# Attention of a decoder trunk: the causal mask inside the row pass, and GpSimd for the scaling of the weights

## The chip, the core and the metric

The kernel is one program on one core of a Trainium2 chip. The metric is the device time of one execution in microseconds (us). A core has five engines with a queue each: TensorE (matmuls; PE in the profile, its weight loads PEld), VectorE (DVE), ScalarE (ACT), GpSimd (POOL) and SyncE (SP), which here issues the transfers. They work in their own order and wait for each other at semaphores. SBUF is the memory on the chip, PSUM the banks that TensorE writes its sums to.

## The reference, cut to what matters

512 tokens of 1024 features go through a Mamba-2 layer and an attention layer, each followed by a SwiGLU mixer. The attention has 16 query heads of 64 features on four shared heads of keys and values, with three branches: compressed blocks, selected blocks and a window. With 512 tokens the selection takes all blocks and the window all keys, so both are causal softmax attention, on keys and values of their own:

```python
s = einsum("bqhgd,bhqnkd->bhgqnk", qr, ks) * scale
p = masked_softmax(s, tok <= t)            # selected blocks
o_sel = einsum("bhgqnk,bhqnkd->bqhgd", p, vs)
...
p = masked_softmax(s, wmask)               # window
o_win = einsum("bhgqk,bkhd->bqhgd", p, vw)
o = g[..., 0:1] * o_cmp + g[..., 1:2] * o_sel + g[..., 2:3] * o_win
```

`g` are gates per token, head and branch. All is float32.

## The kernel before

The work is written in a tile language. A planner orders the instructions of VectorE, GpSimd and SyncE by its own costs; in the attention loop the orders of TensorE and ScalarE are those of the program text (`manual_schedule`).

The loop runs over 32 units (t, b): eight pairs of heads t, and for each the four tiles b = 3, 2, 1, 0 of 128 queries. A query tile b has n = 128 (b + 1) keys, since later ones are masked. A unit has four rows of scores per query: two heads on two branches. In `nsa`, one turn of the loop does this, in TensorE's order:

- `scores` of the next unit: per bank two matmuls (high and low part of the queries, L995 and L996), then a matmul that adds the mask of the last 128 keys (L998; the mask is a bfloat16 tile of 0 and -1e30 times the identity). VectorE takes the negated extreme of each row (L1000), ScalarE the exponential with the row's sum (L1005). For b = 3 and 2 a bank holds one row of scores (`per` is 1), for b = 1 two, for b = 0 all four.
- `turn_over` of this unit: TensorE transposes the weights (L1036) to PSUM, in two parts; VectorE copies the first part back (L1042), ScalarE the second (L1040). Two PSUM banks (`mi`) serve all turns, so the second part waits for the copies of the first.
- between the two parts, `av` of the unit before: the weights times the values (L1053), and after b = 0 the compressed branch (L888).
- some steps of `queries` of the pair t + 2 (`fills`: 1, 1, 2 and 5 steps of three matmuls for b = 3, 2, 1, 0), which end with the rotation: a shuffle (L705) and products on VectorE (L708), a product on GpSimd (L706), a sum (L710), the high part on ScalarE (L712), the low part on VectorE (L714). Then four transfers spread the result over the partitions (L844), and `scores` of (t + 1, 3) waits for them.
- `normalise` of the next unit: reciprocal of the sums (L1011), times the gates (L1013), then the four scalings of the weights (L1016), all on VectorE.
- for even t, steps of `compressed`, with matmuls of their own (L943).

Of the kernel before, what the change touches and what calls it, by code (L numbers as in the profile page):

```python
# [9 lines left out]
F32 = mybir.dt.float32  # L10
# [4 lines left out]
OP = mybir.AluOpType  # L15
# [25 lines left out]
class Weights:  # L41
    """A matrix as a stream of 128x128 blocks, eight to a transfer, each split exactly in two."""
# [21 lines left out]
    def held(self):  # L64
        """The next eight blocks, to be kept for longer."""
        assert self.left == 0
        hi, lo = self.kern.split_unit(self.dram[self.unit], held=True)
        self.unit += 1
        return [(hi[:, i * P:(i + 1) * P], lo[:, i * P:(i + 1) * P]) for i in range(8)]


class Kernel:
# [19 lines left out]
    def banks(self, n, i=0):  # L92
        """n banks to accumulate in; of two or four, the ones of i differ."""
        if n == 2:
            return [self.acc(), self.acc()] if i == 0 else [self.seg(), self.seg()]
        return [self.acc() for _ in range(min(n, N_ACC))] + [self.seg() for _ in range(n - N_ACC)]
# [11 lines left out]
    def split(self, hi, lo, src, bias=None):  # L108
        """hi + lo is src (+ bias) with all of its bits, each part exact in float32r."""
        nc = self.nc  # L110
        if bias is None:
            nc.scalar.activation(hi, src, AF.Copy)  # L112
            nc.vector.tensor_tensor(out=lo, in0=src, in1=hi.bitcast(F32), op=OP.subtract)  # L113
        else:
            nc.scalar.activation(hi, src, AF.Identity, bias=bias)
            nc.vector.scalar_tensor_tensor(out=lo, in0=src, scalar=bias, in1=hi.bitcast(F32),
                                           op0=OP.add, op1=OP.subtract)
# [19 lines left out]
    def linear(self, weights, x, ps=None):  # L137
        """One tile of 128 output features; x is a list of (hi, lo) per input tile."""
        ps = self.acc() if ps is None else ps
        for k, (xh, xl) in enumerate(x):  # L140
            wh, wl = weights.next()
            self.mm3(ps, wh, wl, xh, xl, k == 0, k == len(x) - 1)
        return ps

    def linear_start(self, weights, x, count, parts):
        """The first tiles of output features, token part by token part, as their inputs come."""
        pss = self.banks(count)
        ws = [weights.held() for _ in range(count)]
        for sl in parts:
            for ps, w in zip(pss, ws):  # L150
                for k, (xh, xl) in enumerate(x):
                    self.mm3(ps[:, sl], w[k][0], w[k][1], xh[:, sl], xl[:, sl], k == 0, k == len(x) - 1)
        return pss

    def mod(self, n, behind=False):
        """Modulation columns 128 n.. : silu(c) @ mod_w + mod_b."""
        nc = self.nc
        raw = self.rawp.tile([P, 1024], F32, name="raw")
        nc.sync.dma_start(raw, self.a["mod"][n])
        i = nc.vector.scalar_tensor_tensor(out=raw, in0=raw, scalar=1.0, in1=self.cs, op0=OP.mult, op1=OP.mult,  # L160
                                           accum_out=self.modc[:, n:n + 1])
        if behind:
            self.tc.keep_in_program_order(i)
        nc.vector.tensor_tensor(out=self.modc[:, n:n + 1], in0=self.modc[:, n:n + 1],
                                in1=self.col("mod_b", n), op=OP.add)
# [8 lines left out]
    def scale_cols(self, gain, mod0, plus):  # L174
        """gain * (plus + modulation) as columns."""
        o = self.const.tile([P, KD], F32, name=f"sc_{gain[0]}_{gain[1]}")
        self.nc.vector.scalar_tensor_tensor(out=o, in0=self.mod_cols(mod0), scalar=float(plus),
                                            in1=self.col(gain[0], gain[1], KD), op0=OP.add, op1=OP.mult)
        return o

    def rsqrt(self, sums, n):
        """1 / sqrt(sums / n + eps) of a few columns."""
# [20 lines left out]
    def rstd(self, sums, n):  # L203
        """1 / sqrt(mean + eps) of sums of squares [feature lane, token], on all partitions, in PSUM."""
        nc = self.nc
        ps = self.mi()
        for t in range(4):
            nc.tensor.matmul(ps[:, t:t + 1], sums[:, t * P:(t + 1) * P], self.ones[:, 0:1], start=True, stop=True)
        y = self.rsqrt(ps[:, 0:4], n)
        ps = self.mi()  # L210
        for t in range(4):
            nc.tensor.transpose(ps[:, t * P:(t + 1) * P], y[:, t:t + 1].to_broadcast([P, P]), self.ident)
        return ps

    def unit_rows(self, x, out):
        """out[t] = x[t] * rstd, for a few tiles of tokens [token, feature]; written over with squares before."""
# [16 lines left out]
    def turned(self, xn, k, count=1):  # L233
        """Feature tiles k.. of rows, with features on partitions, in PSUM."""
# [8 lines left out]
    def modulate(self, h, src, scale, shift, k, sl):  # L243
        """h = (hi, lo) of src * scale + shift."""
# [8 lines left out]
    def rows(self, cols):  # L253
        """Columns of features as rows of 1024, on all partitions."""
# [17 lines left out]
    def mm3_rows(self, ps, x, t, wh, wl, start, stop):  # L272
        """Adds to ps, [token, 512 features], what input tile x gives for token tile t."""
# [6 lines left out]
    def project_out(self, dram, x, x_src, gain, x_dst, first=None, after=None, mods=(), held=()):  # L280
        """x_src + gain * rmsnorm(x @ weights), [token, feature]. The second half of the features is done in two
        token parts, and what follows on a part (after) goes on while the other is multiplied. Without first, both
        halves of the features are."""
# [29 lines left out]
        for i in range(2):  # L313
# [19 lines left out]
            # one token tile ends before the other  # L333
# [62 lines left out]
    def before(self, gain, mod0, keep=None):  # L396
        """What follows on the residual stream: the modulated norm, to go on with; and its tiles."""
# [46 lines left out]
    def conv(self, ps, j):  # L444
        """Causal convolution of four taps of channel tile j."""
# [8 lines left out]
    def steps(self, ps, c):  # L454
        """softplus, cumulated decays and what hangs on them, from the raw steps [32 heads, tokens]."""
# [139 lines left out]
    def ssd(self, g, bt, ct, xs, w, h, c, zs):  # L595
        """The eight heads of group g: [2 heads x 64, tokens] tiles, gated and normalised."""
        nc = self.nc
        # C B per chunk: [source, target] blocks (0,0) (0,1) of each chunk, then (1,1) of each
# [15 lines left out]
        # tokens on partitions: steps times x, and with the decay to the end of chunk 0  # L614
# [84 lines left out]
    def rope(self, ps, factor, flat, out):  # L699
        """Rotated 512 tokens of two heads to out; flat gets the unrotated ones."""  # L700
# [16 lines left out]
    def compress_in(self, ps, t, t2):  # L717
        """Two heads' tokens to [(token parity, feature), head, token pair]."""
# [7 lines left out]
    def compress_blocks(self, t2, which):  # L726
        """The blocks with their position embedding, split: per half of their rows [row lane, row, head, block]."""
# [14 lines left out]
    def compress(self, blocks, which, c):  # L742
        """silu(blocks @ w1) as [hidden, 2, (head, block)], blocks with their position embedding."""
# [15 lines left out]
    def nsa(self, came, x_src, x_dst):  # L759
        nc = self.nc  # L760
        hk, xt = came
        with ExitStack() as es:
# [3 lines left out]
            nc.vector.tensor_copy(out=self.mask_q, in_=c("mask_q"))  # L766
            rot = self.big()
# [8 lines left out]
            # keys and values  # L776
# [36 lines left out]
            # gates  # L813
# [13 lines left out]
            # queries, two heads at a time  # L827
# [107 lines left out]
    def compressed(self, flat, kc, gates, kv, c, o):  # L935
        """Gated weights of the compressed blocks for the four heads of kv: [(head, block), query]."""
# [33 lines left out]
    def scores(self, qs, ks, t, b):  # L970
        """Unnormalised causal weights [query, key] of the queries of tile b, of two heads on both branches."""
# [12 lines left out]
        for j in range(4 // per):  # L984
            bank = self.seg()
            for i in range(j * per, (j + 1) * per, min(per, 2)):
# [9 lines left out]
                nc.tensor.matmul(v, q[:, 1, bs], k, start=False, stop=False, skip_group_check=True)  # L996
                for x in ([v[:, 0], v[:, 1]] if per > 1 else [v]):
                    nc.tensor.matmul(x[:, n - P:n], self.identb, self.mask_q, start=False, stop=True,  # L998
                                     skip_group_check=True)
            nc.vector.tensor_reduce(nm[:, j * per:(j + 1) * per],  # L1000
# [7 lines left out]
    def normalise(self, unit, gates, t, b):  # L1008
# [6 lines left out]
        for i, p in enumerate(unit["p"]):  # L1015
            nc.vector.tensor_scalar(p, p, d[:, i:i + 1], None, op0=OP.mult)  # L1016

    def turn_over(self, unit, b, part):
        """Weights with keys on partitions; part 0 by VectorE, part 1 by ScalarE."""
# [26 lines left out]
    def weigh(self, po, unit, vt, t, b, first):  # L1046
        """Adds to po what the queries of tile b get, for the heads 2 t and 2 t + 1."""
# [54 lines left out]
def _cols(v):  # L1102
    """A vector as columns of 128."""
# [3 lines left out]
def _blocks(w, order):  # L1107
    """Blocks (k, n) of w in that order, eight to a unit: [unit, 128, 8 * 128]."""
# [12 lines left out]
def _halves(w):  # L1121
    """Blocks of a half of the columns after the other's."""
# [3 lines left out]
def _rows(w, width):  # L1126
    """Row tiles of w, each [128, n], put side by side to units of 1024 columns."""
# [59 lines left out]
```

## Time and profile before

| | us |
|---|---|
| runs shown | 1564.48, 1565.19, 1568.77 (median 1565.19) |
| span of the profiled execution | 1564.4 |
| TensorE busy | 1515.3 (97%) |
| VectorE busy | 989.5 (63%) |
| ScalarE busy | 701.9 (45%) |
| GpSimd busy | 20.4 (1%) |
| attention loop, in the span | 937 to 1140 |

The span runs from the first to the last instruction of the profiled execution; its own device time is not listed beside it, and the runs are other executions. Busy time is a share over stages with different limits, so what a change in the loop is worth has to be read from the loop. Matmuls overlap in their pipeline and their ends are modelled, so starts are safer to read than durations. "x4" in a timeline merges four instructions.

### The profile page before, as it was taken

The page shows a single profiled execution, that of the slowest core. Times are in us where ns is not written, and L with a number is a line of the kernel's source. Part 1 is how long each engine was busy: PE and PEld are TensorE (multiplying, and loading weights), DVE is VectorE, ACT ScalarE, POOL GpSimd, SP SyncE. Part 2 cuts the span into 40 slices and gives each one's busy share as a digit, 9 for nine tenths or more (in the row PEclk, how much of TensorE's full clock was granted, in tenths as well). Part 3 has the DMA queues.
Part 4 walks back from the last instruction along what each step waited for, and adds up shares of the span by engine and source line. Part 5 has one row for each costly group of instructions (what it writes and reads, how often), then busy time and mean ns, then how long its engine had stood idle before and what let it go on. Part 6 is the DMA issues. An engine that isn't in the chain of part 4 may idle for free.

```text
span 1564.4 us, 20765 instructions
## 1 busy us (share of the span) xinstructions
PE 1515.3 (97%) x8014; PEld 1216.9 (78%) x8014; DVE 989.5 (63%) x1800; ACT 701.9 (45%) x1228; POOL 20.4 (1%) x27
## 2 busy tenths in 40 slices
PE   6999999999999999999999989999999999999997
PEld 4767676777889788888878877777688888888886
DVE  7856676778585788872367578888856333333246
ACT  4564746565364222322356465655645332222243
POOL 0000000000000000000000100000000000000000
PEclk9999999999999999999999999999999999999999
DMA  8422141334763888873466443122144122232254
GB/s 303 152 68 68 41 135 46 117 121 156 257 211 109 280 296 285 297 269 101 167 215 210 108 149 94 48 75 68 42 175 149 41 95 94 95 106 95 95 202 148
DMA packets 65125, 226.11 MB, mean 145 GB/s; under 512 B 7809, under 2 KB 9345, under 8 KB 65026
## 3 DMA queue, kind: packets, MB, share of 16 engines
q1 hardware_dynamic: 64738, 224.53, 43.5%
q8 instruction: 63, 1.03, 0.3%
q14 instruction: 36, 0.29, 0.1%
q10 hardware_dynamic: 288, 0.25, 0.1%
HBM read 204.83 MB, written 8.39 MB: 136 GB/s over the span
## 4 chain that ended last, share of the span: by engine, by line
PE 77%; DVE 9%; DMA 8%; ACT 3%; issue 2%; SPq 1%; POOL 0%; DVEq 0%; ACTq 0%; POOLq 0%
PE acc L133 12%; PE acc L134 12%; PE acc L135 12%; PE seg L276 5%; PE seg L278 5%; PE seg L277 5%; PE acc L278 3%; PE acc L276 3%; PE acc L277 3%; DMA raw<-in_mod_dram 2%; DMA raw<-in_ffn_in_dram 2%; DVE w L113 2%; PE mi L1036 2%; DMA b<-b 2%; PE acc L1053 2%
## 5 line engine op out<-in xcount | busy, mean ns | idle before, releaser
L113 DVE TENSOR_TENSOR w<-raw,w 128x1024 fp32r<-128x1024 f32 x233 | 288.0, 1237 | 260.0 <-ACT w L112 259.3
L112 ACT ACTIVATE w<-raw 128x1024 fp32r<-128x1024 f32 x233 | 245.9, 1057 | 369.4 <-PE seg L278 120.5
L133 PE MATMUL acc<-b,w 128*128 128x512 f32 x976 | 386.0, 397 | 3.2 <-DVE t L450 1.0
L134 PE MATMUL acc<-b,w 128*128 128x512 f32 x976 | 384.0, 393 | 0.0
L135 PE MATMUL acc<-b,w 128*128 128x512 f32 x976 | 383.5, 393 | 0.1
L133 PEld LDWEIGHTS acc<-b,w 128*128 128x128 f32 x976 | 183.3, 188 | 43.1 <-issue 4.1
L135 PEld LDWEIGHTS acc<-b,w 128*128 128x128 f32 x976 | 183.7, 188 | 39.8 <-issue 1.7
L134 PEld LDWEIGHTS acc<-b,w 128*128 128x128 f32 x976 | 183.8, 188 | 36.9 <-issue 0.7
L160 DVE SCALAR_TENSOR_TENSOR raw<-raw,b 128x1024 f32<-128x1024 f32 x112 | 136.1, 1221 | 19.1 <-DMA raw<-in_mod_dram 18.4
L276 PE MATMUL seg<-w,b 128*128 128x512 f32 x340 | 132.9, 391 | 0.0
L278 PE MATMUL seg<-w,b 128*128 128x512 f32 x340 | 132.7, 390 | 0.0
L277 PE MATMUL seg<-w,b 128*128 128x512 f32 x340 | 132.4, 389 | 0.0
L1005 ACT ACTIVATE b<-seg,nm 128x512 f32<-128x512 f32 (+3 forms) x128 | 66.0, 525 | 52.5 <-DVE nm L1000 49.8
L112 ACT ACTIVATE b<-t 128x512 fp32r<-128x512 f32 (+1 forms) x108 | 55.2, 529 | 47.8 <-DVE t L426 38.5
L277 PEld LDWEIGHTS seg<-w,b 128*128 128x128 f32 x340 | 63.8, 188 | 13.3
L278 PEld LDWEIGHTS seg<-w,b 128*128 128x128 f32 x340 | 63.8, 188 | 13.2
L276 PEld LDWEIGHTS seg<-w,b 128*128 128x128 f32 x340 | 63.9, 188 | 12.7
L426 DVE TENSOR_TENSOR t<-t,acc 128x512 f32<-128x512 f32 x40 | 27.4, 685 | 63.3 <-PE acc L135 63.3
L425 ACT ACTIVATE t<-acc 128x512 f32<-128x512 f32 x40 | 23.7, 593 | 95.3 <-PE acc L135 95.3
L113 DVE TENSOR_TENSOR b<-t,b 128x512 fp32r<-128x512 f32 (+1 forms) x108 | 59.2, 567 | 9.2 <-ACT b L112 8.9
L277 PE MATMUL acc<-w,b 128*128 128x512 f32 x164 | 64.0, 390 | 0.0
L278 PE MATMUL acc<-w,b 128*128 128x512 f32 x164 | 64.0, 390 | 0.0
(300 smaller groups left out, 2390.1 us busy)
## 6 DMA issues: line engine op xcount, KB each, us to landing
raw<-in_mod_dram SPq DMA_DIRECT2D x112, 512.0 KB, 4.5
raw<-in_ffn_in_dram SPq DMA_DIRECT2D x88, 512.0 KB, 4.5
raw<-in_ffn_out_dram SPq DMA_DIRECT2D x66, 512.0 KB, 3.3
raw<-in_ssm_in_dram SPq DMA_DIRECT2D x41, 512.0 KB, 3.4
raw<-in_ssm_out_dram SPq DMA_DIRECT2D x24, 512.0 KB, 4.3
b<-b SPq DMA_DIRECT2D x32, 256.0 KB, 4.5
raw<-in_kv_dram SPq DMA_DIRECT2D x12, 512.0 KB, 4.2
raw<-in_q_dram SPq DMA_DIRECT2D x9, 512.0 KB, 5.5
```

The costliest lines, as they stand in the source:

```text
L112: nc.scalar.activation(hi, src, AF.Copy)
L113: nc.vector.tensor_tensor(out=lo, in0=src, in1=hi.bitcast(F32), op=OP.subtract)
L133: nc.tensor.matmul(ps, wh, xh, start=start, stop=False)
L134: nc.tensor.matmul(ps, wh, xl, start=False, stop=False)
L135: nc.tensor.matmul(ps, wl, xh, start=False, stop=stop)
L160: i = nc.vector.scalar_tensor_tensor(out=raw, in0=raw, scalar=1.0, in1=self.cs, op0=OP.mult, op1=OP.mult, accum_out=self.modc[:, n:n + 1])
L276: nc.tensor.matmul(ps, x[0][:, ts], wh, start=start, stop=False)
L277: nc.tensor.matmul(ps, x[0][:, ts], wl, start=False, stop=False)
L278: nc.tensor.matmul(ps, x[1][:, ts], wh, start=False, stop=stop)
L1005: nc.scalar.activation(p[i], bank[:, at:at + n], AF.Exp, bias=nm[:, i:i + 1], accum_out=d[:, i:i + 1])
L1036: nc.tensor.transpose(ps[:, i * n + a * P:i * n + (a + 1) * P], unit["p"][j * per + i][:, a * P:(a + 1) * P], self.ident)
L1053: self.nc.tensor.matmul(po[64 * i:64 * i + 64, bs], vt[a][:, r * 256 + kv * 64:r * 256 + kv * 64 + 64], unit["w"][2 * i + r][:, a * P:(a + ...
```

## The change

For the query tiles b = 3 and 2, the mask's matmul is left out. One instruction of VectorE, `tensor_tensor_reduce`, replaces the reduction: it reads the scores in PSUM and a mask of 512 columns in SBUF (zeros, and the triangle in the last 128 columns), adds them, negates the sum, writes it to SBUF in the place of the weights, and takes the smallest of the row. ScalarE's exponential then works in place on SBUF with a scale of -1. Tiles b = 1 and 0 keep mask and reduction. In `normalise` of all tiles, the scaling of the weights goes from VectorE to GpSimd. The wide mask is built once, by GpSimd. The diff also strips comments and docstrings, left out here.

```diff
@@ nsa
             nc.vector.tensor_copy(out=self.mask_q, in_=c("mask_q"))
+            self.mask_w = keep.tile([P, 512], F32, name="mask_w")
+            nc.gpsimd.memset(self.mask_w[:, 0:384], 0.0)
+            nc.gpsimd.tensor_copy(out=self.mask_w[:, 384:512], in_=c("mask_q"))
@@ scores
                 nc.tensor.matmul(v, q[:, 0, bs], k, start=at == 0, stop=False, skip_group_check=True)
-                nc.tensor.matmul(v, q[:, 1, bs], k, start=False, stop=False, skip_group_check=True)
-                for x in ([v[:, 0], v[:, 1]] if per > 1 else [v]):
+                nc.tensor.matmul(v, q[:, 1, bs], k, start=False, stop=per == 1, skip_group_check=True)
+                for x in ([v[:, 0], v[:, 1]] if per > 1 else []):
                     nc.tensor.matmul(x[:, n - P:n], self.identb, self.mask_q, start=False, stop=True,
                                      skip_group_check=True)
+            if per == 1:
+                nc.vector.tensor_tensor_reduce(out=p[j], in0=bank[:, 0:n], in1=self.mask_w[:, 512 - n:512],
+                                               scale=-1.0, scalar=3.0e38, op0=OP.add, op1=OP.min,
+                                               accum_out=nm[:, j:j + 1])
+                nc.scalar.activation(p[j], p[j], AF.Exp, bias=nm[:, j:j + 1], scale=-1.0, accum_out=d[:, j:j + 1])
+                continue
             nc.vector.tensor_reduce(nm[:, j * per:(j + 1) * per],
@@ normalise
         for i, p in enumerate(unit["p"]):
-            nc.vector.tensor_scalar(p, p, d[:, i:i + 1], None, op0=OP.mult)
+            nc.gpsimd.tensor_scalar(p, p, d[:, i:i + 1], None, op0=OP.mult)
```

## Rows read from the trace of the kernel before

**Rows 1.** Busy time by stretch: stretch, length, PE, PEld, DVE, ACT, POOL (instructions), clock.

```profile
937.00:1140.00 203.00, 194.25 (x1554) 148.44 (x1552) 171.45 (x415) 120.78 (x344) 10.17 (x7) 0.98 0.25 68
```

**Rows 2.** Waits, 937 to 1140 us: who for whom, total us, times, longest.

```profile
ACT b L1005 <- DVE nm L1000: 49.8, 41, 5.4
...
PEld mi L1036 <- DVE b L1042: 9.3, 20, 2.5
...
PE seg L995 <- DMA b<-b: 6.3, 8, 1.4
```

**Rows 3.** Timeline of TensorE, scores of (2, 2): start, us, engine, line, operands.

```profile
1001.42 0.33 PE L995 MATMUL seg<-b,b 128*128 128x384 f32 x1
...
1001.77 0.23 PE L998 MATMUL seg<-mask_q,identb 128*128 128x128 bf16 x1
...
1003.27 0.93 PE L1036 MATMUL mi<-ident,b 128*128 128x128 f32 x7
```

**Rows 4.** Timeline of TensorE, scores of (2, 3).

```profile
993.46 0.39 PE L995 MATMUL seg<-b,b 128*128 128x512 f32 x1
...
993.92 0.23 PE L998 MATMUL seg<-mask_q,identb 128*128 128x128 bf16 x1
...
994.51 0.23 PE L998 MATMUL seg<-mask_q,identb 128*128 128x128 bf16 x1
995.76 0.47 PE L995 MATMUL seg<-b,b 128*128 128x512 f32 x1 [1.03 <-DMA b<-b]
...
996.97 0.60 PE L1036 MATMUL mi<-ident,b 128*128 128x128 f32 x4
```

**Rows 5.** Groups by line and shape, 937 to 1140 us: busy us, mean ns, idle before.

```profile
L1005 ACT ACTIVATE b<-seg,nm 128x512 f32<-128x512 f32 x32 | 21.7, 684 | 22.5 <-DVE nm L1000 20.1 <-DVE cd L962 2.4
...
L1000 DVE TENSOR_REDUCE nm<-seg 128x1 f32<-128x384 f32 x32 | 15.7, 551 | 3.4 <-PE seg L998 3.4
...
L954 ACT ACTIVATE t<-t 128x512 f32<-128x512 f32 x4 | 2.5, 622 | 0.0
```

**Rows 6.** Timeline of VectorE in the first mixer: a pass with an accumulator.

```profile
511.47 1.23 DVE L160 SCALAR_TENSOR_TENSOR raw<-raw,b 128x1024 f32<-128x1024 f32 x1
512.62 0.08 DVE L160 DVE_READ_ACCUMULATOR raw<-raw,b 128x1 f32 x1
```

**Rows 7.** Timeline of VectorE at t = 1, 2 and 7.

```profile
983.28 0.17 DVE L1011 RECIPROCAL d<-d 128x4 f32<-128x4 f32 x1
...
983.94 0.15 DVE L1013 TENSOR_TENSOR d<-d,gates 128x4 f32<-128x4 f32 x1
984.13 1.41 DVE L1016 TENSOR_SCALAR b<-b,d 128x384 f32<-128x384 f32 x4
...
987.59 0.68 DVE L714 TENSOR_TENSOR b<-t,b 128x512 fp32r<-128x512 f32 x1
988.19 0.16 DVE L1011 RECIPROCAL d<-d 128x4 f32<-128x4 f32 x1
...
998.78 0.18 DVE L1011 RECIPROCAL d<-d 128x4 f32<-128x4 f32 x1 [0.92 <-ACT b L1005]
...
1129.18 0.17 DVE L1011 RECIPROCAL d<-d 128x4 f32<-128x4 f32 x1
```

**Rows 8.** Groups of GpSimd, and one row of its timeline.

```profile
L863 POOL MEMSET b<- 128x1024 f32 x1 | 0.9, 949 | 0.0
...
1029.89 1.28 POOL L706 TENSOR_TENSOR t<-t,b 128x512 f32<-128x512 f32 x1 [23.51 <-DVE t L705]
```

**Rows 9.** Timeline of TensorE: the turnings of (1, 2), (1, 1) and (7, 2).

```profile
984.71 0.84 PE L1036 MATMUL mi<-ident,b 128*128 128x128 f32 x6
...
989.59 0.61 PE L1036 MATMUL mi<-ident,b 128*128 128x128 f32 x4
...
1131.05 0.82 PE L1036 MATMUL mi<-ident,b 128*128 128x128 f32 x6
```

## The prediction

> **What bounds the kernel now.** I read the page first: TensorE is busy for 97% of the span (the table above), so a gain has to come out of its queue or out of one of its waits. All that the diff touches lies in the attention loop, from 937 to 1140 us. The table by stretches [rows 1] says that in these 203 us TensorE is busy for 194, VectorE for 171, ScalarE for 121 and GpSimd for 10: VectorE is the second tightest, GpSimd nearly empty. The list of waits in that stretch [rows 2] says where TensorE stands still: 9.3 us in 20 waits for the copies of `turn_over` (L1042, VectorE) and 6.3 us in 8 waits for the transfers that spread the rotated queries (b<-b, into `scores`). No wait for the scaled weights (L1016) is in it. ScalarE's 50 us of waiting for the row extremes cost nothing as long as the weights come in time. So the loop is bound by TensorE's program order, with two latencies of VectorE showing through. The sum is made against the span, 1564.4 us; the three runs have a median of 1565.2, and I take the 0.8 above it as what lies around the span.
>
> **The mask's matmuls.** Per pair of heads t, the tiles b=3 and b=2 have four masks each: 64 of the 128 go; b=1 and b=0 keep theirs. A mask costs more than its own columns, since the pair behind it runs less smoothly. At b=2 the first, undisturbed pair of score matmuls takes 1001.42 to 1001.77, 0.35 us; four pairs with their masks take 1001.42 to 1003.27, 1.85 [rows 3]. Without masks 4 x 0.35 = 1.40: 0.45 saved. At b=3 an undisturbed pair takes 993.46 to 993.92, 0.46; the first two with masks take 1.09 (993.46 to 994.51, and 0.04 for the mask), the last two 1.21 (995.76 to 996.97) [rows 4]. Against 0.92 for two this is 0.17 + 0.29 = 0.46. Over 8 t's some 7.3 us leave TensorE's queue. How much of it reaches the end depends on what TensorE meets next.
>
> Behind the scores of b=2 it is the wait for L1042 in the unit (t,3): VectorE has to do four row passes, two steps of the rotation and then the copies, and TensorE waits for them already. Coming 0.45 sooner only lengthens this wait. Only the first pass can start earlier, as it then waits for the second score matmul and not for the mask (0.15), and I count on that in the even t's: 4 x 0.15 = 0.6 us.
>
> **The new row pass.** A reduction of 384 columns takes 551 ns [rows 5]. The new instruction reads scores in PSUM and the mask in SBUF, writes the masked and negated scores and leaves the extreme in an accumulator. Nothing in the trace has this form. The nearest row is L160, which reads two tensors in SBUF, writes one and accumulates: 1024 columns hold the engine from 511.47 to 512.62, 1.15 us, and the read of the accumulator adds 0.08 at most [rows 6]. That is 1.12 ns a column, 0.43 for 384 and about 0.5 with its fixed part: no more than the reduction, so I take nothing. The other end is half that rate, 0.4 us more at 384 columns: a rival below. The exponential then reads SBUF instead of PSUM. At 512 columns ScalarE's exponentials take 684 ns from PSUM with their sum and 622 from SBUF without [rows 5]; either sign is hidden, as ScalarE is busy for 121 of 203 us and waits for the pass as before. The PSUM bank comes free sooner, for which nobody waits now. Building the wide mask (one memset, one copy on GpSimd) lies far ahead of the loop and costs nothing; not ready at the first score it would cost its own length, under 1 us.
>
> **The scaling on GpSimd.** 128 instructions leave VectorE; four chained ones of 384 columns are 1.41 us there [rows 7]. No row shows a scaling on GpSimd. From below: a memset writes 1024 columns in 0.95 us, 0.93 ns a column, so 0.36 for 384. From above: L706 multiplies two tensors of 512 columns in 1.28, so 0.98 for 384 with its fixed part [rows 8]. Scaling reads one stream and writes one; I take about the middle, 0.70 at 384, 0.9 at 512, 0.5 at 256, 0.3 at 128. The load is 8 x 4 x 2.4 = 77 us of 203, so capacity is no question, only lateness. The Trainium skill (GPSIMD Engine Reference, Engine selection) speaks against the move: elementwise work on a tile belongs on VectorE, since GpSimd is about twice as slow with two inputs, though near line rate with one; no run here shows the case of one. Its best measured loop, 1.8 cycles an element (same page, Elementwise — side-by-side cycle accounting), would as an estimate give 0.58 us for 384 columns, and the sum 0.7 us less stall than I charge below.
>
> Where is lateness covered? Unit (t,3)'s weights are scaled behind the fill steps: at t=2 the reciprocal is at 998.78 and the turning at 1003.27 [rows 7, 3], 4.5 us, enough for 0.4 and four of 0.9. b=0's are covered by the next t's scores. The tight place is b=2 at odd t, where no work for the compressed branch lies between. At t=1 the reciprocal starts at 983.28, the gate product ends at 984.09, and TensorE takes the first weights at 984.71 [rows 7, 9]: 1.43 us from reciprocal to need, the second weights 0.37 later. On GpSimd the first are ready 0.81 + 0.05 + 0.70 = 1.56 after the reciprocal, the second after 2.26, 0.46 too late; then the previous unit's product covers the rest. The four odd t's have 1.4 to 1.9 us [first and last in rows 7, 9]; the last of them loses nothing: 1.4 us in all. The last unit of all, whose four scalings (4 x 0.3 against some 0.9) nothing covers, loses 0.4.
>
> **What VectorE gives back.** At t=1, L1016 stands for 1.41 us before two reductions, two copies and L714, which releases the transfer of the next queries at 987.59 [rows 7]. Without L1016 only the copies wait, for weights that come at 985.5 and their turning: L714 goes at about 986.7, 0.9 sooner. I take 0.8. The transfers land as much sooner. TensorE's waits for them are 0.41 to 1.03 in four units (one is in [rows 4]) and 1.4 and 2.3 in two that wait twice. Of wait and masks together a unit gains the smaller of wait + 0.46 and 0.8 + 0.29, since a transfer that is still late hides the first two masks: 1.09 in four units, 0.96 and 0.87 in two, 0.46 where there is no wait and 0.3 in the prologue: 7.0 us.
>
> **Sum.** 7.0 + 0.6 - 1.4 - 0.4 = 5.8 us. The span becomes 1558.6, the median 1559.4. Over 0.3% (4.7 us) is about what a measurement can tell from no change here, so this is just faster.
>
> **Rivals.**
>
> *GpSimd at the two-tensor rate: no change.* With 0.98 at 384 the second weights come 2.83 us after the reciprocal: 1.03 late at three odd t's, 0.6 at the last, 3.7 in all; L714 gains only 0.45, so the 7.0 become 5.2. At b=1, with 1.40 us from 988.19 to 989.59 [rows 7, 9], 0.2 is lost in five units; the last unit loses 0.7. 5.2 + 0.6 - 3.7 - 1.0 - 0.7 = 0.4: 1564.8. For it: the only GpSimd arithmetic in the trace has this rate. Against: it has a second input. Chance 0.16.
>
> *The masks are hidden anyway: no change.* VectorE's order is planned anew; if L714 stays behind later row passes, the transfers land as now, the b=3 masks save only their last two (8 x 0.29 = 2.3) and the b=2 ones wait for L1042: 2.3 + 0.6 - 1.8 = 1.1: 1564.1. For it: the waits of [rows 2] lie just behind the saved matmuls. Chance 0.15.
>
> *GpSimd slower than its cover: slower.* If a scaling of 384 columns takes x, odd t's lose 2x - 0.94 each. At x = 1.4 that is 4 x 1.86 = 7.4; b=1 loses some 4, the last unit 2; the transfers gain nothing, so the masks give 2.9: 10.5 us slower, 1576. It decides from x = 1.0 on. Against: it is beyond any row. Chance 0.13.
>
> *The new pass at half rate: slower.* 0.4 more in each of four passes lengthens the wait for L1042 by 1.6 in every (t,3), 8 x 1.6 = 13 us, against 5.8: 7 slower, 1572. For it: the form is new. Against: L160 accumulates at full rate [rows 6]. The Trainium skill (Vector Engine (DVE) Microarchitecture Reference, Points that are easy to get wrong) has it that a pass of this family runs at half throughput with two float32 sources in SBUF; L160 is just that and shows no halving, so the trace disagrees, and here one source is in PSUM. Chance 0.10.
>
> **Chances and range.** The forecast has 0.46; its own range, with the scaling between 0.36 and 0.85 and L714 gaining 0.4 to 1.2, is 1555 to 1562. Faster: 0.46. Same: 0.16 + 0.15 = 0.31. Slower: 0.13 + 0.10 = 0.23. From 1554 to 1572 the range leaves out the upper half of the last two rivals and little else.
>
> **What would show it.** In the changed profile: score matmuls of b=2 at 0.35 us a pair; the new pass near 0.55 us at 384 columns; a GpSimd scaling of 0.4 to 0.9 us there; waits of the turning (L1036) for GpSimd of about 2 us in all, at odd t; waits for the spread transfers down from 6.3 to some 2; those for L1042 not down. It is wrong if the scaling takes over 1 us, if the new pass takes twice its reduction, or if GpSimd's rotation product (L706) lands behind four scalings, so that L710 and VectorE's queue wait for it.

## The result, and the profile after

The changed kernel takes 1580.14 us (median of 4 runs, 1577.77 to 1582.48); the kernel before, run beside it, 1564.84. The ratio is 1.0094, 95% interval 1.0071 to 1.0117: some 15 us slower, and outside the range. The profiled execution has a span of 1575.9 us.

The page of the changed kernel, busy time of each engine over the span:

```profile
PE 1514.5 (96%) x7950; PEld 1218.2 (77%) x7950; DVE 955.5 (61%) x1736; ACT 705.9 (45%) x1228; POOL 166.4 (11%) x157
```

VectorE gave up 34 us and GpSimd took 146. The groups of GpSimd, by shape (busy us, mean ns of one, idle time before and what ended it):

```profile
L1026 POOL TENSOR_SCALAR b<-b,d 128x512 f32<-128x512 f32 x32 | 50.7, 1601 | 49.7 <-ACT b L1050 25.7 <-PE seg L999 24.0
L1026 POOL TENSOR_SCALAR b<-b,d 128x384 f32<-128x384 f32 x32 | 41.6, 1318 | 7.3 <-DVE d L1023 7.3
L1026 POOL TENSOR_SCALAR b<-b,d 128x256 f32<-128x256 f32 x32 | 34.0, 1078 | 3.5 <-DVE d L1023 3.2 <-issue 0.3
L1026 POOL TENSOR_SCALAR b<-b,d 128x128 f32<-128x128 f32 x32 | 20.2, 647 | 9.2 <-DVE d L1023 3.5 <-ACT b L1050 3.4 <-DVE cd L963 2.4
```

A scaling of 384 columns takes 1.32 us on GpSimd, where the prediction took 0.70 and had 0.98 as its bound from above. The new row pass and the exponential behind it, same view, engines VectorE and ScalarE:

```profile
L1008 ACT ACTIVATE b<-b,nm 128x512 f32<-128x512 f32 x32 | 22.8, 715 | 18.4 <-DVE nm L1005 14.4 <-DVE cd L965 4.0
L1005 DVE CUSTOM_DVE_ANT_0 b<-seg,mask_w 128x512 f32<-128x512 f32 x32 | 20.9, 688 | 10.3 <-PE seg L999 8.8 <-POOL b L1026 1.4
L1008 ACT ACTIVATE b<-b,nm 128x384 f32<-128x384 f32 x32 | 19.3, 604 | 4.3 <-DVE nm L1005 3.9 <-POOL b L1026 0.4
L1005 DVE CUSTOM_DVE_ANT_0 b<-seg,mask_w 128x384 f32<-128x384 f32 x32 | 15.9, 556 | 7.3 <-PE seg L999 7.2
```

The pass costs what the reduction cost (556 ns against 551 at 384 columns [rows 5]). The waits of the changed kernel from 937 to 1140 us (engine and line, what it waited for; us in all, times, longest):

```profile
PEld mi L1046 <- POOL b L1026: 25.6, 40, 1.4
...
PE mi L1046 <- POOL b L1026: 12.6, 18, 0.9
...
DVE t L710 <- POOL t L706: 7.3, 7, 2.8
...
PE seg L998 <- DMA b<-b: 2.1, 1, 2.1
```

The turning (L1046) now stands for the scaled weights, a wait that [rows 2] doesn't have. (One stand shows both with the weight loads, PEld, and with the matmuls behind them, PE; the two sums overlap and are not added below. Where an expectation gives one number for the waits for the copies, it is their sum.) The timeline of the unit (1,2), where the prediction placed its 0.46 us of lateness, GpSimd, TensorE and VectorE in turn (start, length, in brackets the idle time before):

```profile
984.87 3.68 POOL L1026 TENSOR_SCALAR b<-b,d 128x384 f32<-128x384 f32 x3 [1.32 <-DVE d L1023]
...
984.65 0.29 PE L1001 MATMUL seg<-mask_q,identb 128*128 128x128 bf16 x2
986.16 0.55 PE L1046 MATMUL mi<-ident,b 128*128 128x128 f32 x3 [1.23 <-ACT b L1015]
987.38 0.55 PE L1046 MATMUL mi<-ident,b 128*128 128x128 f32 x3 [0.67 <-POOL b L1026]
...
986.75 0.56 DVE L1052 COPY b<-mi 128x384 f32<-128x384 f32 x1 [1.08 <-PE mi L1046]
...
988.44 0.68 DVE L714 TENSOR_TENSOR b<-t,b 128x512 fp32r<-128x512 f32 x1
```

The first three scalings take 3.68 us, 1.23 each. TensorE has its last scores in at 984.9 and stands 1.23 and 0.67 us for the first two rows of weights (the first wait is put down to L1015, but what ends at 986.1 is GpSimd's first scaling). VectorE is idle, so L714 goes at 988.44: later than before, not sooner.

For the comparisons below, *loop* is the time from the start of the first score matmul to that of the last two matmuls of the compressed branch (one line of the timeline), read from each profile's timeline. The windows view over just that stretch, before and after (length, then busy us of TensorE, its weight loads, VectorE, ScalarE and GpSimd; TensorE's granted clock):

```profile
937.60:1142.12 204.52, 195.78 (x1577) 149.61 (x1575) 173.02 (x417) 122.05 (x345) 10.17 (x7) 0.98 0.25 67
```

```profile
936.98:1152.30 215.32, 194.94 (x1508) 151.49 (x1506) 138.69 (x353) 125.71 (x345) 155.09 (x135) 0.98 0.24 68
```

The loop is 10.8 us longer, and TensorE's idle time in it grows from 8.7 to 20.4 us. The spans differ by 11.5, so nearly all of the loss in the profiled executions is in the loop. That leaves two questions: is it the scaling, and where did the masks' 7 us go?

### The profile page after: what moved, and what is told of

Read it like the earlier page. It is cut to its first block, busy times and chain, and to the rows that moved or that the text cites. A ratio compares the mean times of both kernels' runs of the same rounds, so it can differ in the third digit from the quotient of the medians.

```text
span 1575.9 us, 20819 instructions
## 1 busy us (share of the span) xinstructions
PE 1514.5 (96%) x7950; PEld 1218.2 (77%) x7950; DVE 955.5 (61%) x1736; ACT 705.9 (45%) x1228; POOL 166.4 (11%) x157
## 5 line engine op out<-in xcount | busy, mean ns | idle before, releaser
L113 DVE TENSOR_TENSOR w<-raw,w 128x1024 fp32r<-128x1024 f32 x233 | 289.2, 1242 | 258.9 <-ACT w L112 256.3
L1026 POOL TENSOR_SCALAR b<-b,d 128x512 f32<-128x512 f32 (+3 forms) x128 | 146.3, 1161 | 69.7 <-ACT b L1050 29.1
L276 PEld LDWEIGHTS seg<-w,b 128*128 128x128 f32 x340 | 63.8, 188 | 12.9
L1046 PE MATMUL mi<-ident,b 128*128 128x128 f32 x320 | 54.3, 287 | 18.1 <-POOL b L1026 14.7
L113 DVE TENSOR_TENSOR b<-t,b 128x512 fp32r<-128x512 f32 (+1 forms) x108 | 59.2, 567 | 9.1 <-ACT b L112 9.1
L277 PE MATMUL acc<-w,b 128*128 128x512 f32 x164 | 64.0, 390 | 0.0
```

The lines of the kernel that those rows point to most:

```text
L276: nc.tensor.matmul(ps, x[0][:, ts], wh, start=start, stop=False)
L277: nc.tensor.matmul(ps, x[0][:, ts], wl, start=False, stop=False)
L1026: nc.gpsimd.tensor_scalar(p, p, d[:, i:i + 1], None, op0=OP.mult)
L1046: nc.tensor.transpose(ps[:, i * n + a * P:i * n + (a + 1) * P], unit["p"][j * per + i][:, a * P:(a + 1) * P], self.ident)
```

## The experiments

### The two halves apart

**e1** is the changed kernel with the scaling back on VectorE; **e2** the kernel before with the scaling on GpSimd.

```diff
 # e1, against after
-            nc.gpsimd.tensor_scalar(p, p, d[:, i:i + 1], None, op0=OP.mult)
+            nc.vector.tensor_scalar(p, p, d[:, i:i + 1], None, op0=OP.mult)
 # e2, against before: the same line the other way
```

> The mask in the row pass alone, scaling back on VectorE. Theory (lateness: a scaling of 384 columns takes 1.24 us on GpSimd, and TensorE waits for it): faster than before by 4 to 8 us, 1557 to 1561; no wait of L1046 for GpSimd, the waits for the spread transfers about as before. Rival (the new pass or VectorE's new order costs the time): 1565 or more, waits for the copies or the passes longer than before.

> The scaling on GpSimd alone, masks by matmul as before. Theory (lateness): slower than before by 15 to 22 us, 1580 to 1587, with 35 us or more of TensorE's waits for GpSimd's scaling. Rival (the new pass costs the time): within 5 us of before.

e1: 1568.27 us against 1565.78, ratio 1.001 (1.0 to 1.0021). e2: 1576.21, ratio 1.0062 (1.0043 to 1.0081). So the scaling on GpSimd is the loss, though 10 us and not the 15 to 22 expected, and the masks in the pass give nothing, where 4 to 8 us were expected. The two halves add up to some 11 us of the 15; the difference lies within the three intervals. e2's waits of TensorE in its loop (213.8 us long):

```profile
PE mi L1036 <- POOL b L1016: 10.7, 21, 1.3
PE mi L1036 <- DVE b L1042: 2.9, 8, 1.2
PE seg L995 <- DMA b<-b: 1.0, 1, 1.0
```

The masks are still matmuls here, and TensorE stands for GpSimd, if for 4 us less than in the changed kernel (14.7 in its whole loop).

### The length of the scaling, its cover, its queue

**e3** lets GpSimd scale only the first 128 columns and leaves the others unscaled. **e4** keeps GpSimd for b = 3 and 0, which the prediction held to be covered, but for the last unit. **e6** moves the rotation's product L706, which stood behind four scalings, to VectorE. All against after:

```diff
 # e3
+            nc.gpsimd.tensor_scalar(p[:, 0:P], p[:, 0:P], d[:, i:i + 1], None, op0=OP.mult)
 # e4
+            eng = nc.gpsimd if b in (3, 0) else nc.vector
+            eng.tensor_scalar(p, p, d[:, i:i + 1], None, op0=OP.mult)
 # e6
-        nc.gpsimd.tensor_tensor(out=sw, in0=sw, in1=self.sin, op=OP.mult)
+        nc.vector.tensor_tensor(out=sw, in0=sw, in1=self.sin, op=OP.mult)
```

> As the changed kernel, but GpSimd scales only the first 128 columns of each row of weights; the other columns stay unscaled. The same 128 instructions, waits and hand-overs, each about 0.60 us. Theory (lateness is the length of the scaling): 1556 to 1562, near the forecast, waits for GpSimd under 5 us. Rival (hand-over between engines, the shared port or the order, not the length): over 1570.

> As the changed kernel, but GpSimd scales only the tiles b=3 and b=0, which have the most cover; VectorE scales b=2 and b=1. Theory (lateness where cover is short): 1558 to 1566, with waits for GpSimd of 5 to 12 us at b=3, where four scalings of 1.55 us stand against some 4.5 us of cover. Rival (any use of GpSimd in the loop costs): over 1570.

> As the changed kernel, but the rotation's product (L706) goes from GpSimd to VectorE, so that neither L710 nor VectorE's queue waits behind four scalings. Theory (TensorE's waits for late weights are the loss): no faster than the changed kernel by more than 2 us, 1577 to 1581, with the waits of L1046 for GpSimd still over 35 us. Rival (the rotation behind the scalings delays VectorE and the next queries): 1568 to 1574.

e3: 1565.47, ratio 0.9997 (0.9984 to 1.0011). With 0.64 us a scaling the 15 us are back, but no more than that: the 1556 to 1562 expected were missed, and the waits for GpSimd are still 10.2 us (weight loads and matmuls), where under 5 were expected. e4: 1575.73, ratio 1.0053 (1.0038 to 1.0068): a miss. Four scalings of 512 columns take 6.4 us on GpSimd, and the 4.5 us between reciprocal and turning at b = 3 that the prediction worked out do not cover them; from 937 to 1140 us the weight loads of the turning still wait 16.0 us for GpSimd and its matmuls stand for 5.8. The time is that of the rival (any use of GpSimd costs), whose reason e9 below takes away. e6: 1579.39, ratio 1.0088 (1.0071 to 1.0105), like the changed kernel and as expected: VectorE's 7.3 us of waiting for L706 cost nothing net.

### What makes the scaling slow

**e5** gives the four rows of a unit four forms on GpSimd: scaled by a column, scaled by a constant, multiplied with a broadcast column, and copied.

```diff
             if i == 0:
                 nc.gpsimd.tensor_scalar(p, p, d[:, i:i + 1], None, op0=OP.mult)
+            elif i == 1:
+                nc.gpsimd.tensor_scalar(p, p, 0.5, None, op0=OP.mult)
+            elif i == 2:
+                nc.gpsimd.tensor_tensor(out=p, in0=p, in1=d[:, i:i + 1].to_broadcast([P, (b + 1) * P]), op=OP.mult)
+            else:
+                nc.gpsimd.tensor_copy(out=p, in_=p)
```

> A measurement: as the changed kernel, but the four rows of a unit meet four forms on GpSimd: the scaling by a column as in the change, a scaling by the constant 0.5, a product with the column broadcast, and a copy in place. Rows 2 and 4 are thereby not scaled by their sums. If the column operand makes the scaling slow, the constant and the copy at 512 columns take 0.5 to 0.8 us and the product 1.28 or more, against 1.55; if every pass of GpSimd that reads and writes costs the same, all are between 1.3 and 1.6.

Its groups on GpSimd:

```profile
L1029 POOL TENSOR_SCALAR b<-b 128x384 f32<-128x384 f32 x8 | 11.0, 1380 | 3.9 <-ACT b L1008 2.0 <-issue 1.1 <-PE acc L1070 0.5
L1027 POOL TENSOR_SCALAR b<-b,d 128x384 f32<-128x384 f32 x8 | 9.9, 1244 | 7.3 <-DVE d L1023 4.1 <-ACT b L1057 2.0 <-PE acc L135 1.2
...
L1031 POOL TENSOR_TENSOR b<-b,d 128x384 f32<-128x384 f32 x8 | 6.6, 827 | 0.0
...
L1033 POOL COPY b<-b 128x384 f32<-128x384 f32 x8 | 4.0, 501 | 0.0
```

Neither expectation came: the instruction is slow with a constant as with a column, the copy is not, and the product, which reads two inputs, is a third shorter than the scaling. (Its time, 1557.49 us in a single run, serves no comparison.) So **e9** to **e12** put the product in its place. e10 also brings the rotation's last step (L714, and with it the spread transfers) one step forward. e11 then leaves rows 1 and 2 to VectorE, so that GpSimd's part is half as long. e12 also puts the rotation's first step behind the first part of the turning.

```diff
 # e9, against after
-            nc.gpsimd.tensor_scalar(p, p, d[:, i:i + 1], None, op0=OP.mult)
+            nc.gpsimd.tensor_tensor(out=p, in0=p, in1=d[:, i:i + 1].to_broadcast([P, (b + 1) * P]), op=OP.mult)
 # e10, against e9
+                    if b == order[1]:
+                        next(behind, None)
                     nxt = units[n + 1] if n + 1 < len(units) else None
 # e11, against e10: i < 2 on VectorE (tensor_scalar), the others as in e9
 # e12, against e11
                         p[nxt] = self.scores(qs[nxt[0]], ks[nxt[0] // 2], nxt[0], nxt[1])
+                    done = self.turn_over(p[t, b], b, 0)
                     if b == order[0]:
                         next(behind, None)
-                    done = self.turn_over(p[t, b], b, 0)
```

> As the changed kernel, with GpSimd's scaling written as a product with the broadcast column: 1.04, 0.83, 0.61 and 0.40 us for 512 to 128 columns by the measurement of forms, instead of 1.57, 1.24, 0.92 and 0.60; nothing else differs. Theory (the length of the scaling is the loss): 9 to 14 us faster than the changed kernel, 1565 to 1571, with waits of L1046 for GpSimd under 20 us instead of 44. Rival (the move to GpSimd costs by its hand-overs or its order): 1575 or more.

> As the run with the product, and L714 with its transfers one unit step sooner. If the transfers still hold TensorE: 3 to 5 us faster than the run with the product. If GpSimd's lateness holds it everywhere: within 2 us of it.

> The pass with the mask, L714 sooner, and the scaling shared: rows 1 and 2 of a unit on VectorE, rows 3 and 4, which TensorE takes after the previous unit's product, on GpSimd as products. Theory (lateness alone is bad, the relief of VectorE is good): no wait for GpSimd over 3 us in all, waits for the copies of the turning below the 23 us of the run with L714 sooner; 1555 to 1560. Rival (any share of GpSimd's costs): slower than the run with L714 sooner, 1562 or more.

> As the shared scaling, and the first step of the rotation (L705, L708) emitted after the first part of the turning, so that VectorE's copies go ahead of it in the units (t,3). Theory (the matmuls saved at b=2 hide behind these copies): the waits for the copies fall by 5 us or more against the shared scaling, and the time by 3 to 6 us, 1551 to 1556. Rival (the copies wait for the row passes, not for the rotation, or the queries come late instead): within 2 us of the shared scaling.

e9: 1565.87, ratio 0.9997 (0.9985 to 1.001); e10: 1562.15, 0.9981 (0.9971 to 0.999); e11: 1561.99, 0.9978 (0.9968 to 0.9987); e12: 1564.01, 0.9986 (0.9975 to 0.9997). e9 and e10 came as expected. e9's waits of TensorE in its loop (201.7 us):

```profile
PE mi L1046 <- DVE b L1052: 7.4, 8, 1.6
PE seg L998 <- DMA b<-b: 3.2, 2, 2.2
PE mi L1046 <- POOL b L1026: 0.6, 2, 0.3
```

One instruction exchanged for another on the same engine, in the same place, with the same inputs: 14 us faster (1580.14 to 1565.87), and the stands for GpSimd are down from 14.7 us to 0.6. That settles the cause of the loss. But e9 only draws level with before, and e11, whose stands for GpSimd are gone altogether, missed its 1555 to 1560. e12's later rotation was no gain over e11, where 3 to 6 us were expected: TensorE's stands for the copies fell from 8.5 to 5.2 us, and those for the rows scaled on VectorE rose from 1.0 to 5.4.

### Where the masks' gain goes

**e7** is e1, and **e8** the kernel before, with the rotation's last step forward as in e10, so that the spread transfers are out of the way. **e13** and **e14** are e7 and e8 with VectorE's scaling cut to one column, so that it has less to do ahead of the copies.

```diff
 # e13 against e7, e14 against e8
-            nc.vector.tensor_scalar(p, p, d[:, i:i + 1], None, op0=OP.mult)
+            nc.vector.tensor_scalar(p[:, 0:1], p[:, 0:1], d[:, i:i + 1], None, op0=OP.mult)
```

> The pass with the mask, scaling on VectorE, and the rotation's low part (L714) with its transfers emitted one unit step sooner, ahead of the row passes of the next unit. Theory (the saved matmuls of b=3 hide behind the spread transfers): the waits for them fall from 11 to under 3 us and the dip of the clock at t=7 goes; 4 to 8 us faster than before, 1557 to 1561. Rival (TensorE then only waits longer for the copies of the turning, or for the passes): 1564 to 1567.

> The kernel before, masks by matmul and scaling on VectorE, with the same earlier L714. Theory: its waits for the spread transfers (6.3 us) go, and nothing else: 2 to 5 us faster than before, 1560 to 1563, so that the pass with the mask is worth another 2 to 4 us with the transfers out of the way. Rival (the transfers were hidden or start no sooner): within 1 us of before.

> The mask in the row pass, the rotation's last step early, and the scaling (VectorE) cut to the first column of each row block, the rest of the scaling left out; so VectorE has some 45 us less to do in the loop and the turned copies come in time. Theory (the masks' matmuls do leave about 7 us of TensorE's queue, but TensorE then waits as much longer for VectorE's copies): the waits for the copies fall from 24 us to under 6, and this kernel is 5 to 7 us faster than the same without the mask in the pass (the other kernel of this pair), about 1546. Rival (the removed matmuls were worth only 2 to 3 us to TensorE, since the pair behind a mask ran beside it): 2 to 3 us faster than the other of the pair.

> The kernel before with the rotation's last step early and VectorE's scaling cut to the first column of each row block, the rest of the scaling left out; the masks stay matmuls. Both theories: the waits for the copies fall from 17.5 us to under 6, and the time to some 1552, 12 us under the kernel before. Theory: 5 to 7 us slower than the other of this pair, which has the mask in the pass. Rival: 2 to 3 us slower.

e7: 1560.83, ratio 0.997 (0.9957 to 0.9983). e8: 1564.04, ratio 0.9978 (0.9967 to 0.9989). e13: 1557.5, ratio 0.9945 (0.9923 to 0.9967). e14: 1556.17, ratio 0.9942 (0.9923 to 0.9961). e7 and e8 are some 5 and 3 us faster than before, as expected; e13 and e14 missed their 1546 and 1552. The intervals of each pair overlap: the masks are worth nothing that these runs resolve. The loops say more. The windows view over the loop, as above, of e1 (whose other side is before), of e8 and e7, of e14 and e13:

```profile
939.18:1141.70 202.52, 189.64 (x1513) 150.45 (x1512) 173.68 (x481) 125.20 (x345) 10.19 (x7) 0.98 0.25 67
```

```profile
940.75:1142.37 201.62, 195.95 (x1578) 149.24 (x1576) 173.36 (x417) 122.33 (x345) 10.91 (x7) 0.98 0.25 67
```

```profile
940.72:1139.82 199.10, 189.76 (x1512) 152.20 (x1511) 173.28 (x481) 124.38 (x345) 10.94 (x7) 0.98 0.25 67
```

```profile
936.99:1129.83 192.84, 189.46 (x1572) 146.09 (x1570) 151.57 (x417) 121.89 (x345) 10.18 (x7) 1.00 0.26 72
```

```profile
943.65:1134.06 190.41, 183.88 (x1509) 148.44 (x1508) 151.76 (x481) 124.76 (x345) 10.21 (x7) 1.00 0.26 73
```

| pair | TensorE busy, less by | loop, shorter by | TensorE idle |
|---|---|---|---|
| before, e1 | 6.1 | 2.0 | 8.7 to 12.9 |
| e8, e7 | 6.2 | 2.5 | 5.7 to 9.3 |
| e14, e13 | 5.6 | 2.4 | 3.4 to 6.5 |

Three times the masks' matmuls leave TensorE 6 us less to do, and three times 3 to 4 us of that come back as idle time. TensorE's stands for VectorE's copies say where. The waits over the loop of before and e1, of e8 and e7, of e14 and e13:

```profile
PE mi L1036 <- DVE b L1042: 2.2, 1, 2.2
PE mi L1046 <- DVE b L1052: 5.3, 7, 3.5
...
PE mi L1038 <- DVE b L1044: 3.8, 6, 2.2
PE mi L1048 <- DVE b L1054: 7.0, 11, 3.4
...
PE mi L1038 <- DVE b L1044: 2.0, 2, 1.6
PE mi L1048 <- DVE b L1054: 4.4, 8, 2.4
```

They are 3.1, 3.2 and 2.4 us longer, out of 4.1, 3.7 and 3.1 us more of idle time. The transfers, for which L998 waited 7.2 us in e1 (6.3 before), are out of the way in e7 and e8. In the changed kernel the stands for GpSimd take the time back. The loop of e2, which has the masks as matmuls:

```profile
935.33:1149.13 213.80, 198.96 (x1572) 148.05 (x1570) 140.64 (x289) 122.82 (x345) 152.91 (x135) 0.98 0.25 68
```

Against it, TensorE has 4.0 us less to do in the changed kernel (194.94), stands 4.0 us longer for GpSimd, and the loop is no shorter (215.32).

e13 and e14 were to take the lateness of the copies away, and did so in part only. A scaling of one column still takes 0.21 us on VectorE, so that its busy time falls by 21.5 us and not by the 45 expected, and the waits for the copies are 13.4 and 9.9 us, where under 6 were expected. Of the 5 to 7 us that the theory gave this pair, the loop shows 2.4. That is the rival's number and not its reason: TensorE's busy time falls by 5.6 us. So TensorE's queue does lose 6 us, and most of what comes back is put down to the copies, as the theory had it. Whether the loop would keep the 6 us without that is not shown, since the copies are late in all six kernels.

At the end of e13 nothing of the 2.4 us is left, and the granted clock is the likely reason: its mean over an execution is 0.994 to 0.996 in e13's six runs and 0.997 to 0.998 in e14's five. As an estimate, 0.0024 of 1557 us is up to 3.7 us. In the profiled executions the clock ahead of the loop is 0.83 from 45 to 55 us and 0.89 from 475 to 490 in e13, and 1.00 in e14; that is up to 3.4 of the 6.7 us by which the starts of the loop differ (936.99 and 943.65). What lowers the clock there is open.

**e15** asks whether VectorE's load, or the scaling's place between the sums and the turning, is what the loop pays for: e13, with the scaling's load put back on data that nobody waits for.

```diff
             nc.vector.tensor_scalar(p[:, 0:1], p[:, 0:1], d[:, i:i + 1], None, op0=OP.mult)
+        for i in range(4):
+            nc.vector.tensor_scalar(self.idle[:, 0:(b + 1) * P], self.mask_w[:, 0:(b + 1) * P], d[:, i:i + 1], None,
+                                    op0=OP.mult)
```

> As the kernel with the mask in the pass, the last rotation step early and the scaling cut to one column, and behind the four one-column scalings of each unit VectorE scales four rows of the mask tile to a scratch tile that nobody reads: VectorE's full scaling load is back, but none of it lies between the sums and the turning. Chain theory (the loop pays for the scaling because the turning waits for it, not because VectorE is loaded): the loop stays within 3 us of 190.4. Load theory (VectorE's queue is what delays the copies and passes): the loop goes back to about 199 and the time to some 1561.

1580.76 us, ratio 1.0108 (1.0091 to 1.0124), and a loop of 214.65: worse than both said. VectorE's timeline in one of the turns (t,3) shows where the planner put the load:

```profile
1032.53 0.55 DVE L1008 CUSTOM_DVE_ANT_0 b<-seg,mask_w 128x384 f32<-128x384 f32 x1
...
1033.00 1.03 DVE L1031 TENSOR_SCALAR idle<-mask_w,d 128x512 f32<-128x512 f32 x1
1033.95 0.54 DVE L1008 CUSTOM_DVE_ANT_0 b<-seg,mask_w 128x384 f32<-128x384 f32 x1
...
1034.43 0.47 DVE L1031 TENSOR_SCALAR idle<-mask_w,d 128x512 f32<-128x512 f32 x1
...
1036.39 1.27 DVE L1058 COPY b<-mi 128x512 f32<-128x512 f32 x2
```

It spread the idle scalings between the row passes, all of them ahead of the copies that TensorE stands for. So the chain theory falls as it was put: work on VectorE costs, whoever reads it, when it lies ahead of passes and copies. It gives no price of the load either. VectorE is busy for 191.3 us of e15's loop, 18 more than in e7, as the one-column scalings stay. In one piece right behind the gate product, as in [rows 7], the full scalings cost the loop 8.7 us (199.10 in e7 against 190.41 in e13), spread between the passes 24. And the 8.7 are not VectorE's alone: 5.9 of them are busy time of TensorE, whose clock is 0.98 in e7's loop and 1.00 in e13's.

## Why the prediction was wrong, step by step

**The scaling on GpSimd** is the step that failed. "From above: L706 multiplies two tensors" was no bound: the scaling has one input and is slower than a product with two. At 384 columns it took 1.24 us in e5 (L1027) and 1.32 on average in the changed kernel, where the sum took 0.70 and the bound was 0.98 [rows 8]. The sentence "it is beyond any row" was true, and was used as if a form without a row could not lie beyond the rows. The rule of the Trainium skill that stood beside it (GPSIMD Engine Reference, Engine selection: near line rate with one input) is contradicted by these rows: VectorE does four scalings of 384 columns in 1.41 us [rows 7], GpSimd one in 1.24. The page's advice to keep elementwise work on VectorE held for this instruction: e1, which has it there, is 12 us faster than the changed kernel.

**The lateness** was reasoned rightly for the odd t's and fed with the wrong duration. The rival "GpSimd slower than its cover" takes 2x - 0.94 for an odd t: 1.54 at x = 1.24; the timeline of (1,2) shows 1.90. It gave 1576 at x = 1.4; the runs took 1580. It had a chance of 0.13. By place, the stands of the turning's matmuls are 5.3 us at b = 2 of the odd t's (6.2 by the rival at 1.24), 3.9 at b = 1 (4) and 1.8 in the last unit (2). The last two are near by luck: most of them follow scalings that were lengthened beside VectorE, of which the prediction had nothing (last section). And 4.4 us lie at b = 3, which was called covered: 3.3 in the first unit, the rest at t = 7. With 1.6 us for each of four scalings it isn't covered, as e4 shows.

**The masks' matmuls** were priced about right, 6 us of TensorE's busy time in three pairs against 7.3. A pair of score matmuls at b = 2 takes the 0.35 us foretold; in the changed kernel's timeline at t = 7:

```profile
1130.63 0.34 PE L998 MATMUL seg<-b,b 128*128 128x384 f32 x1
1130.81 0.34 PE L999 MATMUL seg<-b,b 128*128 128x384 f32 x1
1130.98 0.33 PE L998 MATMUL seg<-b,b 128*128 128x384 f32 x1
```

**How much of it reaches the end** failed as well: 7.6 in the sum, 2.0 of the loop and nothing at the end in e1. Most of the 7.0 in it hung on L714 going 0.8 us sooner, and in the changed kernel it went later. Without that this is the rival "the masks are hidden anyway", whose 1.1 us is near. The prediction's own sentence, that the time saved at b = 2 "only lengthens this wait" for L1042, holds in e1: the longest stand for the copies grows from 2.2 to 3.5 us, and 6 short ones are added. One reading under it was wrong, though: the 9.3 us in 20 waits of [rows 2] are those of the weight loads. TensorE's matmuls stood for the copies once, for 2.2 us; their other stands only began when the masks left.

**What VectorE gives back** was the third miss. With the scaling on GpSimd as a product, VectorE is busy for 141 us of the loop in place of 174, and the loop is 0.8 us shorter (e1 202.5, e9 201.7); with the transfers early, 0.1 (e7 199.1, e10 199.0). Cut to one column, the scaling gives 8.7 (e13), a part of it by the clock. The relief of VectorE's queue is there, and it may be that a chain of four GpSimd instructions between sums and turning (4 x 0.83 us in place of 1.41 [rows 7]) takes it back. That fits the rows, but e15, which was to test it, put the load in another place, so it is argued and not shown.

**The waits foretold**: those for the transfers did fall, from 6.3 us [rows 2] to 2.1, but with TensorE held up by GpSimd and L714 no sooner; those for the copies (L1052), said not to fall, fell as well, from 9.3 us to none in the list for the weight loads and from 2.2 to 1.2 for the matmuls. The product L706 did land behind scalings and held L710 for 7.3 us, which was named as a sign of failure; e6 shows that it cost nothing.

**The new row pass** was right: 556 and 688 ns, as the reduction. So was the exponential: 25 to 31 ns longer from SBUF with its sum, 604 and 715 ns, and hidden.

The best of the kernels that leave nothing out are e7, e8, e10 and e11, 3 to 5 us under before with intervals that overlap. What they share is not the change under study but the rotation's last step brought forward (e8 has that alone).

## What to carry to other kernels

A form of instruction without a row has no upper bound from another form, even one that reads more: give a move to a barely used engine a rival without a ceiling, and work out at which duration it decides. Before counting matmuls that leave a busy TensorE, ask what it meets next in its order: here over half of the saved time came back as idle time, for the most part in longer stands for one engine's copies. And an engine's spare capacity says little where the moved work lies in a chain that TensorE waits for.

## What was not expected of the hardware

On GpSimd a float32 scaling costs more a column than a product of two inputs: from the means of 128 and 512 columns in e5, (1565 - 656) / 384 = 2.37 ns a column, against (1041 - 400) / 384 = 1.67 for the product with a broadcast column and (610 - 302) / 384 = 0.80 for a copy. That a scaling by a constant takes 1.38 us at 384 columns shows that reading the column is not what costs. The Trainium skill (GPSIMD Engine Reference, Elementwise — side-by-side cycle accounting) gives 2.6 cycles an element, measured on `tensor_tensor`. At the 1.2 GHz that the page states for this engine this would be, as an estimate, 2.17 ns a column, which is near the scaling, and too much for product and copy, where the measured figures count.

The same scaling also takes longer beside VectorE. In the changed kernel 28 of the 32 scalings of 256 columns take 0.92 us. The other four take 1.96 to 2.28, and each starts while VectorE is in L113, with L958 behind it: products with both inputs in SBUF. The first of the four, and the stand of TensorE behind it:

```profile
966.29 1.22 DVE L113 TENSOR_TENSOR w<-raw,w 128x1024 fp32r<-128x1024 f32 x1
966.65 2.17 POOL L1026 TENSOR_SCALAR b<-b,d 128x256 f32<-128x256 f32 x1
967.43 0.69 DVE L958 TENSOR_TENSOR t<-t,b 128x512 f32<-128x512 f32 x1
...
968.88 0.44 PE L1046 MATMUL mi<-ident,b 128*128 128x128 f32 x2 [0.78 <-POOL b L1026]
```

The stands behind these four, and behind one such scaling in the last unit, are 4.4 of the 14.7 us that TensorE stands for GpSimd. No run takes VectorE's products away, so this is what the trace shows side by side.

TensorE's granted clock fell to half behind some stands. The windows view of the changed kernel, where L998 had waited 2.09 us for a transfer and began again at 1125.67:

```profile
1120.00:1125.00 5.00, 3.01 (x32) 2.08 (x28) 4.93 (x13) 2.12 (x10) 3.56 (x4) 1.00 0.94 246
1125.00:1127.50 2.50, 1.83 (x4) 1.39 (x5) 0.90 (x3) 1.29 (x4) 1.28 (x3) 0.64 0.04 15
1127.50:1130.00 2.50, 2.50 (x23) 1.99 (x22) 1.13 (x6) 2.11 (x5) 0.10 (x1) 0.68 0.00 0
1130.00:1132.50 2.50, 2.28 (x16) 2.01 (x14) 1.67 (x7) 1.61 (x4) 2.50 (x2) 1.00 0.00 0
```

The clock is at its higher level (2.4 GHz) before, at the lower one (1.2 GHz) for a part of two slices, and back after 1130; the two slices together lose at most 2.5 x (0.36 + 0.32) = 1.7 us. The loops of all kernels but e5, e13 and e14 have one or more such stretches, so a wait that is removed can be worth more than its length. Length alone doesn't decide it: in the changed kernel's first unit the clock fell behind four stands of 0.66 to 0.89 us for GpSimd, and e13's 2.44 us for the copies, in the same unit, had no fall behind it.
